# An expert layer's fixed first pass: 64 and 32 rows picked by products, in place of 128 gathered rows

## The chip, the cores and the metric

The kernel runs on one core of a Trainium2 chip. The metric is the device time of one execution in microseconds; a median of a few runs is given, and beside it the time of one execution that the hardware profiler took.

## The reference

Two layers run one after the other on a sequence of 512 tokens of width 1024, all in fp32. The first is a gated mixer (two causal convolutions, a linear recurrence, an output projection). The second adds 16 meta tokens, runs two kinds of attention, projects, and normalises; then comes the part that matters here, a mixture of 32 experts with four experts for each token:

```python
logits = h @ w_router + b_router
top_val, top_idx = lax.top_k(logits, 4)
gates = jax.nn.softmax(top_val, axis=-1)
# for each token and each of its four experts e:
hgu = h[tok] @ w_gate_up[e] + b_gate_up[e]          # 1024 -> 2048
glu, lin = minimum(hgu[::2], 7), clip(hgu[1::2], -7, 7)
act = glu * sigmoid(1.702 * glu) * (lin + 1)
out[tok] += gate * (act @ w_down[e] + b_down[e])    # 1024 -> 1024
```

A last layer norm over the residual and this sum gives the output. Every expert has 8 MB of gate-up and 4 MB of down weights, and all 32 experts are read.

## The kernel before, in words

**Order of the work.** The kernel is written with a manual schedule: each engine runs its instructions in the order in which the program emits them. After attention, an output projection (the loop over `hf` and `i`, around L1466) writes the residual rows `hr` in four blocks of 128 tokens. Beside it each block is normalised (`stats1`, `norm1`, `affine1`), written to DRAM as `h1_d` and `acc_d`, and the router's logits and the four best experts are found (`logits_T`, `logits`, `top4`). Products of the selection with a triangle give each token's place within its expert (`posb`) and the experts' counts; `Pk` orders the experts by count, and `pm_i` holds the order as whole numbers, from which SP reads the addresses of the weights.

**Passes.** Experts are worked through in 32 passes. Pass 0 is always expert 0 (`STATIC`), so its weights can be loaded before the order is known. Passes 3 and 9 (`PAIRS`) take the two largest experts in two tiles of 128 and 32 rows; the next largest have 128 rows, the passes in `SMALL` 64 and those in `TINY` 32. What does not fit is done by a loop at the end (`further_tiles`). A pass has eight gate-up units and four down units, each one load of 1 MB. The down units of pass b - 1 follow the gate-up units of pass b; functions listed by `beside(b)` run before (`before`) or in the middle of (`midst`) the unit with their number: `place`, `fetch` and `gather` find and fetch the rows of the next pass, `xpose` and `xparts` transpose them, `glu`, `at_T` and `at_parts` make the activation and its transpose, `finish` scales and scatters.

**Precision.** A tile of 128 rows uses weights split into two fp32r parts, high and low (ScalarE copies, VectorE subtracts, L142 and L143), and three products for each (L1930, L1941). Tiles of 64 and 32 rows use the raw fp32 weights, with the columns of the array divided in two or four (`small_products`, L1912).

**Weights and buffers.** `Weights` keeps a list of loads in order and a list of free raw buffers of 1 MB. `split` turns a raw buffer into a split one (there are three, of two halves each) and frees the raw one, whereupon the next load is issued on SP; a raw unit frees its buffer with `release` after its products. In the expert stage there are twelve raw buffers, three of which lie where the router's tiles lay before and become free with them.

**Pass 0 before the change.** A one-hot of expert 0's places (`onehot`) times the token numbers gives the indices (`rows_at`); `rows_of` gathers the 128 rows from `h1_d` by an indirect DMA; `xpose` and `xparts` transpose and split them. Twelve warming products of no use (`warm`) stand ahead of the transposes on TensorE. `order()` permutes places and gates by the order of the experts, in steps after the units of pass 0; `late_gates` then finds the gates of pass 0.

Of the kernel before, what the change touches and what calls it, by code (L numbers as in the profile page):

```python
# [9 lines left out]
F32 = mybir.dt.float32  # L10
# [4 lines left out]
OP = mybir.AluOpType  # L15
# [4 lines left out]
S = 512  # L20
# [14 lines left out]
STATIC = 1  # L35
PAIRS = (3, 9)
# [5 lines left out]
def _tables():  # L42

    f = np.float32
    inv = (f(10000.0) ** (-np.arange(0, 64, 2, dtype=f) / f(64))).astype(f)
    pos = np.concatenate([np.arange(NM, NK), np.arange(NM)]).astype(f)
    t = np.arange(S)
    row = np.concatenate([t // 64, np.full(NM, -1)]).astype(f)
    col = np.concatenate([t % 64, np.arange(NM)]).astype(f)

    def block(p):
        ang = (p[None, :] * inv[:, None]).astype(f)
        c, s = np.cos(ang).astype(f), np.sin(ang).astype(f)
# [24 lines left out]
    for r, q_ in enumerate([*PAIRS, *large, *[q_ for q_ in SMALL if q_ not in TINY], *TINY, *range(STATIC)]):  # L78
        moe[:, q_] = r
        moe[:, 32 + q_] = 160 if q_ in PAIRS else 32 if q_ in TINY else 64 if q_ in SMALL else 128  # L80
    moe[:, 64] = p // 64
    moe[:, 65] = p // 32

    least = np.arange(NE) + 131072.0 * (np.arange(NE) < STATIC)
    moe[:, 66] = least[p % NE]
    moe[:, 67:67 + NE] = least

    moe[:64, 68 + NE] = moe[64:, 70 + NE] = 1.0
    return {"t_rope": np.ascontiguousarray(rope.astype(f)), "t_sq": sq, "t_moe": moe}


class Weights:
# [3 lines left out]
    def __init__(self, nc, pools, slots):  # L96
        self.nc, self.slots = nc, list(slots)
        self.parts = [(pools, f"wpart{i}") for i in range(2)]
        self.todo, self.raw, self.part = [], [], []
        self.last, self.used = 0, 0  # L100

    def add(self, *loads, split=True, n=2048, pieces=1, late=0):

# [44 lines left out]
        self.rest = [lambda i=i: piece(i) for i in range(1, pieces)]  # L148

    def release(self, slot):  # L150
        self.slots.append(slot)
        self.issue()

    def ahead(self, n):
        while len(self.part) < n and self.ready():
# [15 lines left out]
def block_kernel(ctx, tc, A, out, dbg=None, upto=99):  # L171
# [118 lines left out]

    PASSES, ni = [], 0
    for p in range(NE):
        k = 1 + (p in PAIRS)
        PASSES.append(list(range(ni, ni + k)))
        ni += k
    NI = ni
# [8 lines left out]

    def paired(p):

        return p not in PAIRS and p not in TINY
# [4 lines left out]
    def add_unit(p, dn, u, of, late=0):  # L313
        def src():
            w = of(p)[dn]
            return rows2(w[256 * u:256 * u + 256, :], paired(p)) if dn else w[128 * u:128 * u + 128, :]
        W.add((kn(2, 1024) if dn else flat, src), split="both" if p in PAIRS else p not in SMALL,
              late=late)

    def add_block(b, of):  # L320
# [1143 lines left out]
    for hf in range(2):  # L1464
        sl_ = slice(512 * hf, 512 * hf + 512)
        wb = [t.rearrange("p (k n) -> p k n", k=4) for t in W.get(1)]  # L1466
        wa = [t.rearrange("p (k n) -> p k n", k=4) for t in W.get(0)]
        for i in range(4):
            pa, pb = psa("pwa"), psa("pwb")
            for g, p_, w in ((1, pb, wb), (0, pa, wa)):  # L1470
                for k in range(4):
                    mm3(p_, [t[:, 4 * g + k, 128 * i:128 * i + 128] for t in osp], [t[:, k, :] for t in w], k == 0, k == 3)
                if hf and i and g:
                    logits_T(i - 1)
                    norm1(i - 1)
            if hf and i:
                logits(i - 1)
            if hf == 0 and i == 0:
                o_scales()
                l1g = bcast(A["ln1_g_2"], pB, "hm")  # L1480
            for g, p_ in ((1, pb), (0, pa)):
                dve.scalar_tensor_tensor(out=hr[:, i, sl_], in0=p_, scalar=rst[:, i, g:g + 1], in1=hr[:, i, sl_],
                                         op0=OP.mult, op1=OP.add)
                if hf and i and g:
                    affine1(i - 1)
            if hf:
                stats1(i)
                if i:
                    top4(i - 1)
                else:  # L1490
                    W.ahead(1)
            elif i == 1:
                biases()
            elif i == 2:
                W.ahead(1)
                next(terms)
            elif i == 3:
                next(terms)
    logits_T(3)
    norm1(3)  # L1500
    logits(3)
# [53 lines left out]
        dve.tensor_copy(out=pi2[:, c0:c1], in_=pi_[:, c0:c1])  # L1555
        return pi2

    def rows_of(pi_, nt=1):
# [9 lines left out]
        w = 128 // nt  # L1568
        xg = xg2[nsl[0] % 2][0:w]
        nsl[0] += 1  # L1570
        pool.indirect_dma_start(out=xg, out_offset=None, in_=h1_d[:, :],  # L1571
                                in_offset=bass.IndirectOffsetOnAxis(ap=ix[0:w], axis=0),
                                bounds_check=S - 1, oob_is_err=False)
# [7 lines left out]
        dve.scalar_tensor_tensor(out=gt, in0=pi_[:, 2:3], scalar=pi_[:, 3:4], in1=pi_[:, 4:5], op0=OP.add, op1=OP.add)  # L1581
        return gt

    oh_ = onehot(posb[:, :, 0:1])
    first = rows_of(rows_at(oh_, lambda i: aux[:, :, i, 0], 0, 2))

    cnt = pK.tile([128, NE], F32, name="cnt")
    pmr = pK.tile([128, NE], F32, name="pmr")
# [178 lines left out]
    def small(n):  # L1767

        if PASS_OF[n] in TINY or PLACES[n][1]:
            return 4  # L1770
        return 2 if PASS_OF[n] in SMALL else 0

    def place(n):
        p, k = PLACES[n]
        pl = posb[:, :, p:p + 1]
        if k:
            pl2 = pM.tile([128, 4], F32, tag="pl2", name="pl2", bufs=2)
            dve.tensor_scalar(out=pl2, in0=posb[:, :, p], scalar1=128.0, scalar2=None, op0=OP.subtract)
            pl = pl2.unsqueeze(2)
        its[n] = {"oh": onehot(pl, small(n) or 1), "cols": lambda i: aux[:, :, i, p], "se": selr[:, p:p + 1].to_broadcast([128, 128]),  # L1780
                  "acc": {}, "ac": {}, "pa": {}, "parts": {}}
# [21 lines left out]
                                         in1=it["pi"][:, 1:2], op0=OP.add, op1=OP.add)  # L1803
        it["gt"] = gates_of(it["pi"])

    def late_gates(n):
        it = its[n]
        it["gt"] = gates_of(rows_at(it["oh"], it["cols"], 2, 5))

    def xpose(n):  # L1810
        it = its[n]
        if small(n):
            it["pt"] = transposed_rows(it["xg"])
        else:
            pt = pss("pxt") if n == 0 else None
            it["pt"] = [transposed(it["xg"], a, pt[:, a, :] if n == 0 else psa("pxt")) for a in range(2)]

    def x_tile():
        return [pM.tile([128, 8, 128], F32R, tag=t, name=t) for t in ("xTh", "xTl")]
# [72 lines left out]
    def small_products(n, dn, u, w, half):  # L1892
# [15 lines left out]
        for k in range(2):  # L1908
# [38 lines left out]
    def beside(b):  # L1947
# [21 lines left out]
                before[9 if b else 8].append((glu, n, 1))  # L1969
        nxt = PASSES[b + 1] if b + 1 < NE else []  # L1970
        if b == 0:
            before[4].append((place, 1))
            midst[4].append((fetch, 1))
            before[5] += [(gather, 1), (late_gates, 0)]
            before[8].append((place, 2))
            midst[7].append((xpose, 1))
            before[8].append((xparts, 1))
        else:
            for j, n in enumerate(nxt):
                if j:  # L1980
# [27 lines left out]
    def further_tiles():  # L2008
# [4 lines left out]
        with tc.For_i(0, total, 1) as it:  # L2013
            with tc.manual_schedule():
# [46 lines left out]

    W.slots += [(pM, f"wraw{RAW + RAWK + i}") for i in range(RAWX)]
    W.prefetch()
    its[0] = {"oh": oh_, "cols": lambda i: aux[:, :, i, 0], "ix": first[0], "xg": first[1],
              "se": selr[:, 0:1].to_broadcast([128, 128]), "acc": {}, "ac": {}, "pa": {}, "parts": {}}
    for p, dn, u in units(1):
        if not dn:
            add_unit(p, dn, u, of, -4)
# [129 lines left out]
```

## Time and profile before

| | |
|---|---|
| median of three runs (lowest to highest) | 1894.53 us (1890.97 to 1894.7) |
| profiled execution | 1889.37 us, span 1887.6 us |
| granted TensorE clock, mean | 0.951 |
| busy: TensorE, VectorE, ScalarE, GpSimd | 1682.0, 1127.2, 752.8, 512.6 us |
| first load of pass 0's weights, first product of pass 0 | 752.96, 819.84 us |
| last load of weights issued | 1831.34 us |

The span runs from the first to the last instruction. Rows of the timeline give the start of a group of equal instructions, its length, its engine (SPq is SP's queue of transfers), its line and operation, the tiles it writes and reads, the shapes and a count. Behind them in brackets stands the time for which the engine was idle before, and what ended that. A matmul of fp32 operands leaves two records, and a record's length includes its way through the array, so the pace of a stream is read from start to start. A granted clock of 1.00 is 2.4 GHz and 0.50 is 1.2 GHz.

### The profile page before, as it was taken

The numbers are of one execution on the slowest core, as the hardware profiler recorded it, in microseconds if no ns is written. First come the engines' busy times: TensorE is split into PE (matmuls) and PEld (weight loads), VectorE is DVE, ScalarE is ACT, GpSimd is POOL, SyncE is SP. The second block draws the span as 40 slices with busy tenths as digits, with TensorE's granted clock in tenths as the row PEclk, the third lists the DMA queues.
The fourth block names the chain that finished last, engine by engine and source line by source line (L and its number), as shares of the span: only waits on it lengthen the run. The fifth ranks groups of instructions, "written<-read, shape, count | busy, mean of one in ns | idle before, by whom it ended". The sixth has DMA issues, their size and how long they took to land. (4 is left out here: it accounts for less than half of the span.)

```text
span 1887.6 us, 22807 instructions
## 1 busy us (share of the span) xinstructions
PE 1682.0 (89%) x8479; PEld 1120.8 (59%) x8479; DVE 1127.2 (60%) x1467; ACT 752.8 (40%) x894; POOL 512.6 (27%) x400
## 2 busy tenths in 40 slices
PE   4899785979998899978999999999999999999885
PEld 3687573758787677854565565666456556642221
DVE  6799983775746555756565466566547545641113
ACT  5233542742335545333354354445335534520001
POOL 3899994550311221311111101110011011110102
PEclk8999897989999899989899999999999999999998
DMA  8322221336131003769999999999999999999993
GB/s 300 90 73 73 78 90 45 111 133 210 59 109 56 1 1 111 296 266 364 379 394 410 399 413 397 394 403 414 418 404 407 406 404 393 405 407 397 407 414 136
DMA packets 127442, 503.49 MB, mean 267 GB/s; under 512 B 15227, under 2 KB 57785, under 8 KB 79713
## 3 DMA queue, kind: packets, MB, share of 16 engines
q1 hardware_dynamic: 115568, 475.24, 63.7%
q0 software_dynamic: 11024, 25.39, 4.9%
q8 instruction: 68, 1.11, 0.2%
q10 hardware_dynamic: 736, 1.38, 0.2%
q14 instruction: 46, 0.37, 0.1%
HBM read 488.56 MB, written 19.84 MB: 269 GB/s over the span
## 5 line engine op out<-in xcount | busy, mean ns | idle before, releaser
L143 DVE TENSOR_TENSOR wlo<-wraw,whi 128x2048 fp32r<-128x2048 f32 (+1 forms) x201 | 456.9, 2282 | 177.8 <-ACT whi L142 172.1
L142 ACT CAST whi<-wraw 128x2048 fp32r<-128x2048 f32 (+1 forms) x201 | 379.5, 1890 | 222.2 <-DMA wraw<-w_down 93.9
L1912 PE MATMUL pg<-wraw,xTs 128*64 128x512 f32 (+1 forms) x1664 | 277.1, 518 | 15.0 <-DMA wraw<-w_gate_up 14.8
L1912 PEld LDWEIGHTS pg<-wraw,xTs 128*64 128x64 f32 (+1 forms) x1664 | 85.5, 126 | 166.2 <-issue 109.8
L1912 PE MATMUL pg<-wraw,ats 128*64 128x512 f32 (+1 forms) x832 | 146.2, 527 | 8.9 <-DMA wraw<-w_down 6.7
L1660 DVE TENSOR_SCALAR lp<-pg 128x512 f32<-128x512 f32 (+1 forms) x47 | 31.1, 661 | 191.9 <-ACT sg L1659 190.3
L563 POOL TENSOR_TENSOR acc<-acc,sparel 128x512 f32<-128x512 f32 x91 | 133.3, 1465 | 7.7 <-ACT acc L552 0.2
L1667 POOL DMA_INDIRECT acc_d<-y,back x20 | 33.1, 1656 | 374.9 <-ACT y L1886 357.1
L1571 POOL DMA_INDIRECT xg<-h_d,ix x34 | 53.9, 1584 | 235.3 <-PE pg L1912 109.8
L1930 PE MATMUL pg<-whi,xTh 128*128 128x512 f32 x416 | 117.1, 403 | 0.4 <-issue 0.4
L1930 PE MATMUL pg<-whi,xTl 128*128 128x512 f32 x416 | 115.8, 400 | 0.0
L1930 PE MATMUL pg<-wlo,xTh 128*128 128x512 f32 x416 | 113.3, 394 | 0.0
L1667 POOL DMA_INDIRECT acc_d<-y,ix x13 | 26.1, 2011 | 309.0 <-ACT y L1889 210.2
L556 DVE SCALAR_TENSOR_TENSOR pc<-v,C,pc 128x512 f32<-128x512 f32 x144 | 101.6, 747 | 2.1 <-ACT pc L552 0.8
L1659 ACT ACTIVATE sg<-pg 128x512 f32<-128x512 f32 (+1 forms) x47 | 25.7, 573 | 183.4 <-PE pg L1912 99.9
L561 POOL TENSOR_SCALAR sparel<-v,C 128x512 f32<-128x512 f32 x91 | 93.8, 1031 | 14.5 <-DVE V L478 5.8
L1930 PEld LDWEIGHTS pg<-whi,xTh 128*128 128x128 f32 x416 | 76.3, 189 | 26.5 <-issue 10.3
L1930 PEld LDWEIGHTS pg<-wlo,xTh 128*128 128x128 f32 x416 | 78.9, 190 | 17.9
L1930 PEld LDWEIGHTS pg<-whi,xTl 128*128 128x128 f32 x416 | 77.3, 190 | 16.6
L1941 PE MATMUL pg<-whi,ath 128*128 128x512 f32 x208 | 73.9, 438 | 12.8 <-ACT whi L142 12.8
L1912 PEld LDWEIGHTS pg<-wraw,ats 128*64 128x64 f32 (+1 forms) x832 | 41.2, 127 | 73.7 <-issue 47.6
L1941 PE MATMUL pg<-wlo,ath 128*128 128x512 f32 x208 | 71.7, 428 | 11.8 <-DVE wlo L143 11.8
(661 smaller groups left out, 3289.3 us busy)
## 6 DMA issues: line engine op xcount, KB each, us to landing
wraw<-w_gate_up SPq DMA_DIRECT2D x256, 1024.0 KB, 20.5
wraw<-w_down SPq DMA_DIRECT2D x128, 1024.0 KB, 21.7
wraw<-w_in SPq DMA_DIRECT2D x17, 1024.0 KB, 5.3
wraw<-w_out SPq DMA_DIRECT2D x8, 1024.0 KB, 6.1
mraw<-mod_w SPq DMA_DIRECT2D x7, 1024.0 KB, 12.5
wraw<-w_in SPq DMA_DIRECT2D x14, 512.0 KB, 5.1
wraw<-pw_w SPq DMA_DIRECT2D x4, 1024.0 KB, 5.2
wraw<-mod_w SPq DMA_DIRECT2D x4, 1024.0 KB, 5.1
```

Source lines behind the costliest of these rows:

```text
L142: self.nc.scalar.copy(out=hi[:, c], in_=t[:, c])
L143: self.nc.vector.tensor_tensor(out=lo[:, c], in0=t[:, c], in1=hi[:, c].bitcast(F32), op=OP.subtract)
L556: dve.scalar_tensor_tensor(out=acc[:, c, :] if j == 29 and not np_ else st_["o"], in0=v[:, j:j + S], scalar=dw_col(j, c), in1=st_["o"], op ...
L561: pool.tensor_scalar(out=pr_, in0=v[:, j:j + S], scalar1=dw_col(j, c), scalar2=0.0, op0=OP.mult, op1=OP.add)
L563: pool.tensor_tensor(out=acc[:, c, :], in0=acc[:, c, :], in1=pr_, op=OP.add)
L1571: pool.indirect_dma_start(out=xg, out_offset=None, in_=h1_d[:, :], in_offset=bass.IndirectOffsetOnAxis(ap=ix[0:w], axis=0), bounds_check=S ...
L1659: act.activation(out=sg, in_=v2[:, :, :, 0], func=AF.Sigmoid, scale=1.702)
L1660: dve.tensor_scalar(out=lp, in0=v2[:, :, :, 1], scalar1=-6.0, scalar2=8.0, op0=OP.max, op1=OP.min)
L1667: pool.indirect_dma_start(out=dst, out_offset=bass.IndirectOffsetOnAxis(ap=ix, axis=0), in_=y, in_offset=None, bounds_check=nt * S - 1, oo ...
L1912: pe.matmul(o, l, t[:, c0:c0 + n_], start=False, stop=u == 3 and k == 1 if dn else u == 7)
L1930: pe.matmul(it["acc"][c // 2][:, c % 2, :], l, r[:, 512 * c:512 * c + 512], start=False, stop=u == 7 and j == 2)
L1941: pe.matmul(it["acc"][2][:, c, :], l, r[:, c0:c0 + 512], start=False, stop=end)
```

## The change

Pass 0 gets two tiles, of 64 and of 32 rows, with raw weights. The limit of expert 0 falls from 128 to 96 rows; what is over goes to the loop at the end. Its rows are no longer gathered: a one-hot of 96 places in fp32 is the moving operand of 32 products, with the normalised rows in `hr` as weights, which give the rows of pass 0 already transposed. The first eight of these products stand ahead of the two products that make the experts' order, the other 24 behind them. ScalarE copies the result into two tiles. `late_rows` finds the scatter addresses and gates of both tiles before unit 3. As pass 0 is not split, `lend` adds the six halves of the split buffers to the free raw buffers after the projection's loop; they are not returned to the list when they are released. A pass of two tiles releases its raw buffer after the second.

```diff
+    def lend(self):
+        self.lent = [(pool, tag + x) for pool, tag in self.parts for x in "hl"]
+        self.slots += self.lent
+        self.prefetch()
...
-        k = 1 + (p in PAIRS)
+        k = 1 + (p in PAIRS or p < STATIC)
...
+    W.lend()
     logits_T(3)
     norm1(3)
...
-    oh_ = onehot(posb[:, :, 0:1])
-    first = rows_of(rows_at(oh_, lambda i: aux[:, :, i, 0], 0, 2))
+    oh0 = xg2[0][:, 0:4 * 96].rearrange("p (i n) -> p i n", i=4)
+    dve.tensor_tensor(out=oh0, in0=iotab[:, 0:96].unsqueeze(1).to_broadcast([128, 4, 96]),
+                      in1=posb[:, :, 0:1].to_broadcast([128, 4, 96]), op=OP.is_equal)
+    first = pss("first")
+    def pick_rows(ks):
+        for k in ks:
+            for i in range(4):
+                pe.matmul(first[:, k // 4, 96 * (k % 4):96 * (k % 4) + 96], hr[:, i, 128 * k:128 * k + 128], oh0[:, i, :],
+                          start=(i == 0), stop=(i == 3))
+    pick_rows(range(2))
...
     pe.matmul(pp1[:, NE:2 * NE], pcol[0:NE, 1:2].to_broadcast([NE, 128]), Pk[0:NE], start=True, stop=True)
+    pick_rows(range(2, 8))
...
-    def late_gates(n):
+    def late_rows(n):
         it = its[n]
-        it["gt"] = gates_of(rows_at(it["oh"], it["cols"], 2, 5))
+        place(n)
+        fetch(n)
+        it["gt"], it["ix"] = gates_of(its[n]["pi"]), rows_of(its[n]["pi"], small(n), False)[0]
+        its[n] = it
...
-        W.release(slot)
+        if n == PASSES[PASS_OF[n]][-1]:
+            W.release(slot)
...
-            before[5] += [(gather, 1), (late_gates, 0)]
+            before[5].append((gather, n1))
+            before[3] += [(late_rows, 0), (late_rows, 1)]
...
     warm(12, bias_p)
-    xpose(0)
-    xparts(0)
+    for n, (tag, c0, w) in enumerate((("xTh", 0, 64), ("xTs", 64, 32))):
+        xp = pM.tile([128, 8, w], F32, tag=tag, name="xTs")
+        act.copy(out=xp.rearrange("p (a k) w -> p a k w", a=2),
+                 in_=first[:, :, 0:4 * 96].rearrange("p a (k w) -> p a k w", k=4)[:, :, :, c0:c0 + w])
```

## Rows read from the trace of the kernel before

**Rows 1.** Windows of the expert stage: us, engines' busy time, PEclk, DMA share, GB/s.
```profile
820.00:860.00 40.00, 34.93 (x258) 25.59 (x259) 23.48 (x38) 17.18 (x15) 3.76 (x2) 0.96 0.65 247
...
1200.00:1400.00 200.00, 191.47 (x897) 116.73 (x889) 117.83 (x123) 89.37 (x79) 21.19 (x13) 0.97 1.02 410
```

**Rows 2.** Windows around the end of pass 3, the same columns.
```profile
934.00:946.00 12.00, 10.49 (x63) 5.00 (x65) 6.31 (x11) 1.84 (x4) 0.00 (x0) 1.00 0.78 279
946.00:960.00 14.00, 13.72 (x163) 7.26 (x160) 6.62 (x10) 8.02 (x11) 2.68 (x2) 1.00 1.02 368
```

**Rows 3.** Timeline of SP's queue: a row write, a down load, a later load.
```profile
800.67 0.32 SPq L1423 DMA_DIRECT2D h_d<-hr  x1
...
810.59 0.33 SPq L117 DMA_DIRECT2D wraw<-w_down  x1
...
937.95 0.33 SPq L117 DMA_DIRECT2D wraw<-w_gate_up  x1
```

**Rows 4.** Timeline of TensorE: pass 0, its end, its down units.
```profile
819.84 1.17 PE L1930 MATMUL pg<-whi,xTh 128*128 128x512 f32 x4 [0.38 <-issue]
...
822.66 1.10 PE L1930 MATMUL pg<-whi,xTh 128*128 128x512 f32 x4
...
844.49 0.68 PE L1645 MATMUL pxt<-sq,xg 32*128 32x32 f32 x8 [2.70 <-DMA xg<-h_d,ix]
...
848.18 1.05 PE L1906 MATMUL pg<-bias_p,se 128*128 128x256 f32 x4
...
860.74 0.72 PE L1941 MATMUL pg<-whi,ath 128*128 128x512 f32 x2
...
866.38 0.68 PE L1645 MATMUL pxt<-sq,xg 64*128 64x64 f32 x8 [1.25 <-DMA xg<-h_d,ix]
...
874.26 0.62 PE L1906 MATMUL pg<-bias_p,se 128*128 128x512 f32 x2
```

**Rows 5.** Timeline of TensorE: passes of 32 and 64 rows, one unit of pass 3.
```profile
855.43 4.96 PE L1912 MATMUL pg<-wraw,xTs 128*32 128x256 f32 x88
...
881.99 7.95 PE L1912 MATMUL pg<-wraw,xTs 128*64 128x512 f32 x36
...
917.95 1.20 PE L1930 MATMUL pg<-whi,xTh 128*128 128x512 f32 x4
...
921.90 1.20 PE L1930 MATMUL pg<-whi,xTh 128*128 128x512 f32 x4
```

**Rows 6.** Timeline of TensorE: narrow products, warming, the entry to pass 3.
```profile
787.42 1.87 PE L1443 MATMUL plog<-rw,xg 128*128 128x32 f32 x16
...
810.66 5.01 PE L198 MATMUL warm<-bias_p 128*128 128x512 f32 x12
...
898.16 1.06 PE L1645 MATMUL pxt<-sq,xg 32*128 32x32 f32 x8 [3.35 <-DVE xTl L215]
899.14 1.94 PE L1912 MATMUL pg<-wraw,ats 128*32 128x256 f32 x16
```

**Rows 7.** Windows of TensorE alone: us, busy time, PEclk, DMA share, GB/s.
```profile
802.00:814.00 12.00, 5.75 (x43) 0.50 0.65 229
814.00:816.00 2.00, 2.00 (x10) 0.75 1.00 414
848.00:850.00 2.00, 1.87 (x13) 0.72 0.00 0
906.00:908.00 2.00, 2.00 (x8) 0.71 1.01 423
```

**Rows 8.** Timeline of VectorE: the first one-hot, indices of two gathers.
```profile
805.04 0.69 DVE L1546 TENSOR_TENSOR oh<-sq,posb 128x512 bf16<-128x512 f32 x1
...
835.68 0.15 DVE L1566 CAST ix<-tok 128x1 int32<-128x1 f32 x1
...
856.56 0.15 DVE L1566 CAST ix<-tok 128x1 int32<-128x1 f32 x1
```

**Rows 9.** Timeline of ScalarE: the first split for pass 3.
```profile
891.75 1.90 ACT L142 CAST whi<-wraw 128x2048 fp32r<-128x2048 f32 x1 [1.17 <-DMA wraw<-w_gate_up]
```

More of the change, by code (lines that the diff above doesn't have):

```diff
@@ L79, in _tables @@
         moe[:, q_] = r
-        moe[:, 32 + q_] = 160 if q_ in PAIRS else 32 if q_ in TINY else 64 if q_ in SMALL else 128
+        moe[:, 32 + q_] = 160 if q_ in PAIRS else 32 if q_ in TINY else 64 if q_ in SMALL else 96 if q_ < STATIC else 128
     moe[:, 64] = p // 64
@@ L99, in __init__ @@
         self.todo, self.raw, self.part = [], [], []
-        self.last, self.used = 0, 0
+        self.last, self.used, self.lent = 0, 0, []
     def add(self, *loads, split=True, n=2048, pieces=1, late=0):
@@ L150, in release @@
     def release(self, slot):
-        self.slots.append(slot)
-        self.issue()
+        if slot not in self.lent:
+            self.slots.append(slot)
+            self.issue()
+    def lend(self):
+        self.lent = [(pool, tag + x) for pool, tag in self.parts for x in "hl"]
+        self.slots += self.lent
+        self.prefetch()
     def ahead(self, n):
@@ L306, in paired @@
     def paired(p):
-        return p not in PAIRS and p not in TINY
+        return p not in PAIRS and p not in TINY and p >= STATIC
     def rows2(w, pairs):
@@ L316, in src @@
             return rows2(w[256 * u:256 * u + 256, :], paired(p)) if dn else w[128 * u:128 * u + 128, :]
-        W.add((kn(2, 1024) if dn else flat, src), split="both" if p in PAIRS else p not in SMALL,
+        W.add((kn(2, 1024) if dn else flat, src), split="both" if p in PAIRS else p not in SMALL and p >= STATIC,
               late=late)
@@ L1556, in rows_at, with rows_of @@
         return pi2
-    def rows_of(pi_, nt=1):
+    def rows_of(pi_, nt=1, gather=True):
         ix = pK.tile([128, 1], I32, tag="ix", name="ix", bufs=6)
@@ L1567, in rows_of @@
             back = pK.tile([128, 1], I32, tag="back", name="back", bufs=6)
[L1568 to L1573, printed above, removed]
+        xg = None
+        if gather:
+            w = 128 // nt
+            xg = xg2[nsl[0] % 2][0:w]
+            nsl[0] += 1
+            pool.indirect_dma_start(out=xg, out_offset=None, in_=h1_d[:, :],
+                                    in_offset=bass.IndirectOffsetOnAxis(ap=ix[0:w], axis=0),
+                                    bounds_check=S - 1, oob_is_err=False)
         if nt > 1:
@@ L1770, in small @@
             return 4
-        return 2 if PASS_OF[n] in SMALL else 0
+        return 2 if PASS_OF[n] in SMALL or PASS_OF[n] < STATIC else 0
     def place(n):
@@ L1777, in place @@
             pl2 = pM.tile([128, 4], F32, tag="pl2", name="pl2", bufs=2)
-            dve.tensor_scalar(out=pl2, in0=posb[:, :, p], scalar1=128.0, scalar2=None, op0=OP.subtract)
+            dve.tensor_scalar(out=pl2, in0=posb[:, :, p], scalar1=64.0 if p < STATIC else 128.0, scalar2=None,
+                              op0=OP.subtract)
             pl = pl2.unsqueeze(2)
@@ L1814, in xpose @@
         else:
-            pt = pss("pxt") if n == 0 else None
-            it["pt"] = [transposed(it["xg"], a, pt[:, a, :] if n == 0 else psa("pxt")) for a in range(2)]
+            it["pt"] = [transposed(it["xg"], a, psa("pxt")) for a in range(2)]
     def x_tile():
@@ L1971, in beside @@
         if b == 0:
-            before[4].append((place, 1))
-            midst[4].append((fetch, 1))
-            before[5] += [(gather, 1), (late_gates, 0)]
-            before[8].append((place, 2))
-            midst[7].append((xpose, 1))
-            before[8].append((xparts, 1))
+            n1, n2 = PASSES[1][0], PASSES[2][0]
+            before[4].append((place, n1))
+            midst[4].append((fetch, n1))
+            before[5].append((gather, n1))
+            before[3] += [(late_rows, 0), (late_rows, 1)]
+            before[8].append((place, n2))
+            midst[7].append((xpose, n1))
+            before[8].append((xparts, n1))
         else:
@@ L2063, in block_kernel @@
     W.prefetch()
-    its[0] = {"oh": oh_, "cols": lambda i: aux[:, :, i, 0], "ix": first[0], "xg": first[1],
-              "se": selr[:, 0:1].to_broadcast([128, 128]), "acc": {}, "ac": {}, "pa": {}, "parts": {}}
+    for n in PASSES[0]:
+        its[n] = {"acc": {}, "ac": {}, "pa": {}, "parts": {}}
+        selectors(n)
     for p, dn, u in units(1):
@@ L2074, in block_kernel @@
     warm(12, bias_p)
-    xpose(0)
-    xparts(0)
+    for n, (tag, c0, w) in enumerate((("xTh", 0, 64), ("xTs", 64, 32))):
+        xp = pM.tile([128, 8, w], F32, tag=tag, name="xTs")
+        act.copy(out=xp.rearrange("p (a k) w -> p a k w", a=2),
+                 in_=first[:, :, 0:4 * 96].rearrange("p a (k w) -> p a k w", k=4)[:, :, :, c0:c0 + w])
+        for k in range(8):
+            its[n]["parts"][0, k] = xp[:, k]
     for b in range(NE + 1):
```

## The prediction, made before the changed kernel ran

> **What bounds the kernel now.** I read the windows first. From 1200 to 1400 us the sixteen DMA engines are busy at a share of 1.02 and move 410 GB/s [rows 1]: the expert stage is a stream of 1 MB weight loads, one per 1.05 MB / 410 GB/s = 2.56 us. At its head there is a hole: share 0.65 and 247 GB/s from 820 to 860 [rows 1]. The change aims at this hole, so the question is whether a microsecond saved there survives to the end.
>
> The second view is the windows of the place where pass 3 ends. The share is 0.78 from 934 to 946 and 1.02 from 946 on [rows 2]. Ahead of 946 every load that could be issued has landed: the queue row at 937.95 [rows 3] comes as a unit of TensorE ends and releases its buffer. So there all twelve weight buffers are full and the loads are paced by TensorE. Pass 3 makes 3.95 us of TensorE work per load (917.95 to 921.90 [rows 5]) against 2.56 us of transfer: here the DMA queue catches up whatever it lost before. Behind 946 the stream has a fixed length. The end of the kernel is then the end of pass 3 on TensorE plus that stream, and what counts ahead of it is TensorE's own chain from the router to pass 3.
>
> **The change part by part.** Times stand against the profiled execution, 1889.37 us (span 1887.6). The median of the runs is 1894.53, 5.2 us higher, and the result is carried over to it.
>
> *Lent buffers.* Six halves of the split buffers become raw buffers at the end of the projection. The loads for them stand in SP's queue behind a row write of the first layer norm at 800.67 [rows 3], so they start at about 801: the three outstanding down loads, of which the last two went at 810.59 and just after [rows 3], and then, once the expert order is known, six loads of pass 1 where three were possible. Pass 0 frees its eight buffers as its units end. By the end of its gate-up pass 6 + 8 = 14 loads of later passes are issued, against 8 before: a lead of 6 x 2.56 = 15 us of transfer. The lent buffers (three with weights of pass 1, three with down units) are not refilled, so at the start of pass 2 both kernels have the same twelve loads ahead, and the lead turns into idle DMA ahead of 934. TensorE's waits between 820 and 934 are on gathers and on VectorE, none on a weight load, so I cost this at nothing; if that is wrong it is the first rival.
>
> *Rows by products.* Removed: a one-hot, four small products, the first gather and its landing, eight transposes and two splits. Added: a one-hot of 4 x 96 and 32 fp32 products of 128x128 by 96, two records each: 64. The one-hot is ready where the old one was, about 805.6 (805.04 plus three quarters of 0.69 [rows 8]). No row shows this shape. The nearest has 128x128 fp32 weights and 32 columns, 16 records in 1.87: 0.117 each [rows 6]. At half clock a record costs twice that: sixteen narrow records took 1.94 at 899.14 [rows 6] where 88 took 4.96 [rows 5], 0.121 against 0.056. The clock is at half when the products begin, 0.50 from 802 to 814 [rows 7].
> The first 16 records: 16 x 0.234 = 3.7, to 809.4. The expert order's two products wait behind them and take about 1.0, to 810.4; the expert numbers are about 1 us later, hidden since pass 1 is not wanted before 848. Then 48 records. The clock rose at 815, 4.3 us after TensorE set to work at 810.66, at 849.1, 4.6 us after 844.49, and once only 9 us after 898.16 [rows 4, 6, 7]. From 805.65 that makes 810 to 815. With the early rise they take 48 x 0.117 = 5.6, to 816.0; with the late one 18 x 0.234 + 30 x 0.117 = 7.8, to 818.2. Behind them stand two transposes (0.2), the twelve warming products, now at full clock (2.8, as a unit of twelve [rows 4]), and pass 0's bias (0.5); the copies of the picked rows lie beside the warming. First gate-up product: 819.5 to 821.7, where it was 819.84 [rows 4], so -0.3 to +1.9. I take +0.5, since two of three rises were early.
>
> *Pass 0 in 64 and 32 rows.* Before, a unit is twelve products, 2.8 us (819.84 to 822.66 [rows 4]). For 64 rows it is 8 records: 36 took 7.95 [rows 5], 1.72 for 8 from start to start. For 32 it is 16 records, 0.90 at 0.056 each; but in pass 3, where they alternate with a wide tile, a unit is 3.95, and 3.95 - 2.8 = 1.15 [rows 5]. I take 1.72 + 1.18 = 2.9. So TensorE does not become faster, though the rows are fewer.
> The Trainium skill, TensorEngine Tiling (Array Packing), section Key Properties, says that a change of tiling mode drains the engine. Each new unit changes mode twice, so this rule speaks against the change; by it a unit is 2.9, without it 2.62 and the gate-up pass 2.2 us shorter. The trace agrees, with 1.15 against 0.90 [rows 5].
> Eight units are 23.2. Added: the second tile's bias 0.65, order products 0.4, three index products 0.75, transposes of pass 1 0.7. The late rows stand before unit 3: their second one-hot waits for some nine short VectorE operations behind the first index product, about 1.7 us of idle TensorE. The gather of pass 1 is asked for at unit 4: its indices are ready 17.4 after the first product. From the indices to the data it took 8.7 (835.83 to 844.49) and the next gather 9.7 (856.71 to 866.38) [rows 4, 8]. So the data are there at 26.1 to 27.1; TensorE comes for them at 25.6, and after the transposes and the last share of 32 the pass ends at 28.0 to 29.0. Before: 819.84 to 848.18, 28.3, with a wait of 2.70 for the same gather [rows 4]. I take 28.5: +0.2 (-0.3 to +0.7). The splits of pass 0 on ScalarE and VectorE are gone; they hid beside TensorE, and what they cost it stands in the next part.
>
> *Pass 1 and pass 0's down units.* The swiglu of two tiles is one behind the other on VectorE, and the 64 comes second: its transpose waits about 1.8 where it waited 0.4; a wait of 1.4 on a split goes, and the copy of pass 1's rows is 0.3 later: +0.3 (0 to +1). The four down units took 13.5, 860.74 to 874.26, with a wait of 1.25 for a gather [rows 4]. Now the products are 4 x 2.9 in place of 4 x 2.8, the bias 0.2 longer, and the wait goes, since the indices of pass 2 no longer stand behind splits: -0.7 (-1.5 to 0).
>
> *Entry to pass 3.* TensorE waits 3.35 at 898.16 for VectorE [rows 6], and the clock is at half until 907 [rows 7]. ScalarE's split before it waited 1.17 for a weight load [rows 9], which now lies ready; but VectorE has other work until it takes that split up. I cost it at 0 (-7.5 to 0).
>
> **Sum:** 0.5 + 0.2 + 0.3 - 0.7 + 0 = +0.3. Profiled 1889.7, median 1894.8: no change.
>
> **The rivals.**
> 1. The lead counts. If the stage is bound by the stream from 813 on, the holes close: 0.35 x 40 = 14.0 [rows 1], 0.22 x 12 = 2.6 [rows 2], and two loads that are there before the order is known, 2 x 2.56 = 5.1: 21.7 in all, 1873. For it: 900 us at full share. Against it: the full buffers of rows 2. Chance 0.12.
> 2. Late weights set the entry to pass 3. With its loads landed early the splits begin earlier, VectorE is free, and the wait of 3.35 and the low clock behind it go (the records of 1.94 and more between 898 and 907 lose some 4 us): -7.5, 1887. For it: the wait of 1.17 on a load just ahead [rows 9]. Against it: VectorE's queue there holds other work. Chance 0.15.
> 3. The clock stays low through picking and warming. Then 64 x 0.234 = 15.0, the order 1.0, transposes 0.4, warming 5.0 as at 810.66 [rows 6], bias 0.9: pass 0 starts at 827.9, +8.1, and the median is 1902. It decides if the rise comes later than about 818. For it: the rise that took 9 us. Against it: picking gives TensorE work almost without a pause. Chance 0.12, with smaller delays of the same kind.
> 4. The change doesn't do what it says: the lent loads wait in SP's queue and start only at 810 with the others. By the argument above that costs nothing and falls into my forecast.
>
> **How the numbers follow.** Forecast 0.61, rivals 0.12, 0.15 and 0.12. What a measurement of this kernel can tell from no change is about 0.2%, 3.8 us. The ends of the forecast's terms add up to -2.1 and +3.6 around nothing, 1892.4 to 1898.1, its own range; for parts of rivals 2 and 3 I leave 0.05 of it below -3.8 and 0.06 above +3.8, 0.50 between. Faster 0.12 + 0.15 + 0.05 = 0.32, same 0.50, slower 0.12 + 0.06 = 0.18. The range takes in rival 2 and all but the end of rival 3, and leaves out rival 1: 1881 to 1901.
>
> **What would show it.** Right: three loads from about 801; more idle DMA between 865 and 946 than now; units of pass 0 of 2.9; a wait on VectorE before unit 3; pass 3's first wide product within 2 us of 903.4, where it is now; the stream after it unchanged. Wrong: a DMA share near 1 from 813 through 946 with the end much earlier (rival 1), no wait ahead of pass 3 (rival 2), a granted clock of 0.5 past 818 (rival 3), or any wait of TensorE on a weight load ahead of 934.

## The result and the profile after

| | before | after |
|---|---|---|
| median of four runs each, same chip | 1892.75 us | 1908.22 us |
| ratio, 95% interval | | 1.0085 (1.0061 to 1.0109) |
| profiled execution, span | 1889.37 us, 1887.6 | 1906.01 us, 1904.2 |

The changed kernel is slower by some 16 us. Forecast was no change, with a range that ended at 1901: the prediction was wrong.

The work ahead of the experts takes a little longer or shorter from one execution to the next, so both profiles are read from one anchor, the last group of logits products: 799.17 before, 800.69 after. TensorE before: the anchor, the first products of pass 2, the end of pass 2 and the first wide product of pass 3 (the columns are start, length, engine, line, operation, tiles, shape, count, and in brackets the idle time ahead and what ended it):

```profile
799.17 1.97 PE L1443 MATMUL plog<-rw,xg 128*128 128x32 f32 x16 [0.73 <-ACT xg L1436]
...
874.82 1.08 PE L1912 MATMUL pg<-wraw,xTs 128*64 128x512 f32 x4
...
889.86 0.50 PE L1906 MATMUL pg<-bias_p,se 128*128 128x256 f32 x2
...
903.37 2.07 PE L1930 MATMUL pg<-whi,xTh 128*128 128x512 f32 x4
```

TensorE after, the start of pass 0:

```profile
800.69 1.97 PE L1450 MATMUL plog<-rw,xg 128*128 128x32 f32 x16 [0.73 <-ACT xg L1443]
...
807.26 3.70 PE L1603 MATMUL first<-xg,hr 128*128 128x96 f32 x16 [1.71 <-DVE cnt L1615]
...
811.88 7.78 PE L1603 MATMUL first<-xg,hr 128*128 128x96 f32 x48
820.73 0.33 PE L1708 MATMUL pord<-sq,posb 128*128 128x128 f32 x1 [1.07 <-ACT xTs L2107]
...
820.92 2.99 PE L205 MATMUL warm<-bias_p 128*128 128x512 f32 x12
...
824.31 1.94 PE L1938 MATMUL pg<-wraw,xTs 128*64 128x512 f32 x8
```

From the anchor to the first wide product of pass 0 it is 23.62 us, where it was 20.67 (819.84 in [rows 4]). The 64 picks took 11.5 us. TensorE, passes 0 and 1 and the down units of pass 0:

```profile
836.18 0.26 PE L1561 MATMUL pidx<-aux,oh 128*128 128x5 bf16 x4 [1.70 <-DVE oh L1550]
836.38 6.44 PE L1938 MATMUL pg<-wraw,xTs 128*64 128x512 f32 x32
...
857.45 0.66 PE L1697 MATMUL pat<-sq,ac 128*128 128x128 f32 x2 [2.01 <-DVE ac L1684]
...
867.24 1.94 PE L1938 MATMUL pg<-wraw,ats 128*64 128x512 f32 x8
```

The wait for the late rows (1.70) is there, and the gather waits of 2.70 and 1.25 [rows 4] are gone. Behind the wait the granted clock stood at half from 837.0 to 840.4, and the 32 records there took 6.44; in experiment 7, behind the same wait with the clock up, they took 4.80. TensorE's window (us, busy time, granted clock, DMA share, GB/s):

```profile
837.00:840.00 3.00, 3.00 (x16) 0.50 0.89 374
```

TensorE from pass 2 to pass 3:

```profile
880.64 1.08 PE L1938 MATMUL pg<-wraw,xTs 128*64 128x512 f32 x4
...
895.27 0.27 PE L1561 MATMUL pidx<-aux,oh 128*128 128x5 bf16 x4 [7.58 <-DVE oh L1550]
895.47 9.38 PE L1938 MATMUL pg<-wraw,xTs 128*64 128x512 f32 x36
904.78 0.50 PE L1932 MATMUL pg<-bias_p,se 128*128 128x256 f32 x2
...
913.08 1.06 PE L1667 MATMUL pxt<-sq,xg 32*128 32x32 f32 x8 [4.34 <-DVE xTl L222]
...
918.29 2.07 PE L1957 MATMUL pg<-whi,xTh 128*128 128x512 f32 x4
```

Here is the loss. In the middle of pass 2 TensorE stands for 7.58 us, in a place where it did not wait at all before, and the 36 records behind it, which took 7.95 [rows 5], take 9.38, since the granted clock fell to half from 891.6 to 898.4. What VectorE and GpSimd did at that time:

```profile
891.58 0.19 DVE L1739 TENSOR_TENSOR xy<-cnt,moe 128x32 f32<-128x32 f32 x1 [12.34 <-DMA acc_d<-y,back]
...
894.52 0.69 DVE L1550 TENSOR_TENSOR oh<-sq,pl 128x512 bf16<-128x512 f32 x1
```

```profile
880.38 1.63 POOL L1689 DMA_INDIRECT acc_d<-y,back  x1 [18.32 <-issue]
885.07 1.57 POOL L1689 DMA_INDIRECT acc_d<-y,back  x1 [3.06 <-DMA acc_d<-y,back]
```

`xy` is the scratch in which the arithmetic for the loop at the end (`further()`) begins. It is allocated under the buffer name `yt`. Before the change nothing used that buffer while pass 0's result was being scattered. Now pass 0 has a second, 32-row tile, and `finish` puts the scaled rows of such a tile into `yt`. So the first small step of `further()` waits until the scatter of these rows has left the buffer: the second of two scatters, which itself waits 3.06 us for the first to land. VectorE works in order, so it stood for 12.34 us, with the one-hot for which TensorE waits behind it in its queue.

SP's queue and the DMA windows of the changed kernel (columns: stretch, length, each engine's busy time, granted clock, DMA share, GB/s):

```profile
802.18 0.32 SPq L1430 DMA_DIRECT2D h_d<-hr  x1
802.60 1.83 SPq L117 DMA_DIRECT2D wraw<-w_down  x3
806.39 0.82 SPq L1430 DMA_DIRECT2D h_d<-hr  x2
807.25 0.94 SPq L1432 DMA_DIRECT2D acc_d<-hr  x2
814.16 7.14 SPq L117 DMA_DIRECT2D wraw<-w_gate_up  x6
```

```profile
810.00:840.00 30.00, 27.23 (x177) 16.98 (x180) 7.14 (x31) 2.51 (x4) 0.00 (x0) 0.84 1.00 403
...
850.00:860.00 10.00, 7.40 (x66) 3.08 (x63) 3.94 (x7) 1.77 (x5) 0.00 (x0) 0.87 0.69 270
...
890.00:900.00 10.00, 4.73 (x20) 1.65 (x22) 7.74 (x22) 0.00 (x0) 1.97 (x2) 0.66 0.43 157
...
960.00:975.00 15.00, 14.72 (x168) 7.58 (x165) 6.70 (x11) 7.87 (x11) 2.68 (x2) 1.00 1.01 373
```

The lending does what it says: the hole from 820 [rows 1] is full up to 840, and the DMA engines idle later instead, in stretches between 840 and 960 (shares of 0.69 and 0.43 in the lines above), until pass 3 has ended.

### The profile page after: what moved, and what is told of

Read it like the earlier page. It is cut to its first block, busy times and chain, and to the rows that moved or that the text cites. A ratio compares the mean times of both kernels' runs of the same rounds, so it can differ in the third digit from the quotient of the medians.

```text
span 1904.2 us, 23177 instructions
## 1 busy us (share of the span) xinstructions
PE 1700.7 (89%) x8680; PEld 1114.0 (58%) x8680; DVE 1103.3 (58%) x1462; ACT 729.5 (38%) x883; POOL 510.1 (27%) x400
## 5 line engine op out<-in xcount | busy, mean ns | idle before, releaser
L143 DVE TENSOR_TENSOR wlo<-wraw,whi 128x2048 fp32r<-128x2048 f32 (+2 forms) x189 | 433.7, 2303 | 169.9 <-ACT whi L142 157.4
L142 ACT CAST whi<-wraw 128x2048 fp32r<-128x2048 f32 (+2 forms) x189 | 356.8, 1889 | 203.5 <-DMA wraw<-w_down 85.5
L1938 PE MATMUL pg<-wraw,xTs 128*64 128x512 f32 (+1 forms) x1856 | 305.1, 519 | 15.6 <-DMA wraw<-w_gate_up 14.8
L1938 PEld LDWEIGHTS pg<-wraw,xTs 128*64 128x64 f32 (+1 forms) x1856 | 93.5, 127 | 183.2 <-issue 124.4
L1938 PE MATMUL pg<-wraw,ats 128*64 128x512 f32 (+1 forms) x928 | 157.7, 519 | 9.6 <-DMA wraw<-w_down 7.1
L1957 PE MATMUL pg<-whi,xTh 128*128 128x512 f32 x384 | 108.0, 403 | 0.0
L1957 PE MATMUL pg<-whi,xTl 128*128 128x512 f32 x384 | 107.7, 402 | 0.0
L1957 PE MATMUL pg<-wlo,xTh 128*128 128x512 f32 x384 | 104.9, 395 | 0.0
L1689 POOL DMA_INDIRECT acc_d<-y,ix x12 | 23.6, 1966 | 288.0 <-ACT y L1915 184.5
L1957 PEld LDWEIGHTS pg<-wlo,xTh 128*128 128x128 f32 x384 | 72.4, 189 | 17.1
L1968 PE MATMUL pg<-wlo,ath 128*128 128x512 f32 x192 | 66.5, 429 | 12.7 <-DVE wlo L143 12.7
L1968 PE MATMUL pg<-whi,ath 128*128 128x512 f32 x192 | 67.2, 433 | 8.9 <-ACT whi L142 8.9
## 6 DMA issues: line engine op xcount, KB each, us to landing
wraw<-w_down SPq DMA_DIRECT2D x128, 1024.0 KB, 21.4
```

The lines of the kernel that those rows point to most:

```text
L142: self.nc.scalar.copy(out=hi[:, c], in_=t[:, c])
L143: self.nc.vector.tensor_tensor(out=lo[:, c], in0=t[:, c], in1=hi[:, c].bitcast(F32), op=OP.subtract)
L1689: pool.indirect_dma_start(out=dst, out_offset=bass.IndirectOffsetOnAxis(ap=ix, axis=0), in_=y, in_offset=None, bounds_check=nt * S - 1, oo ...
L1957: pe.matmul(it["acc"][c // 2][:, c % 2, :], l, r[:, 512 * c:512 * c + 512], start=False, stop=u == 7 and j == 2)
L1968: pe.matmul(it["acc"][2][:, c, :], l, r[:, c0:c0 + 512], start=False, stop=end)
```

## The experiments

The table is read from each kernel's TensorE timeline: from the anchor to the first wide product of pass 0, to that of pass 3, and from there to the end of the span.

| kernel | to pass 0 | to pass 3 | pass 3 to end | ratio to before (95%) |
|---|---|---|---|---|
| before | 20.7 | 104.2 | 984.2 | 1 |
| after | 23.6 | 117.6 | 985.9 | 1.0085 (1.0061 to 1.0109) |
| 1 own scratch | 23.5 | 107.4 | 983.4 | 1.0022 (1.0012 to 1.0032) |
| 2 before, the wait alone | 20.5 | 111.8 | 982.5 | 1.0039 (1.0026 to 1.0053) |
| 3 before, delay ahead of pass 2 | 20.6 | 108.1 | 983.5 | 1.0019 (1.0007 to 1.0031) |
| 4 before, delay ahead of pass 5 | 20.5 | 102.3 | 983.3 | 0.9994 (0.9982 to 1.0005) |
| 5 before, picking alone | 26.3 | 109.9 | 987.1 | 1.0035 (1.0020 to 1.0049) |
| 6 own scratch, rows gathered | 27.0 | 111.3 | 983.8 | 1.0041 (1.0024 to 1.0058) |
| 7 own scratch, no warming | 21.4 | 103.8 | 984.7 | 0.9999 (0.9983 to 1.0016) |
| 8 own scratch, three lent | 23.5 | 108.0 | 984.9 | 1.0010 (0.9999 to 1.0022) |
| 9 as 7, clock held up | 22.3 | 108.2 | 983.5 | 1.0018 (1.0005 to 1.0031) |
| 10 as 9, second tile later | 22.8 | 104.9 | 983.1 | 1.0011 (1.0000 to 1.0021) |
| 11 as 10, lent behind the row writes | 17.3 | 97.8 | 985.1 | 0.9983 (0.9971 to 0.9995) |
| 12 as 7, lent behind the row writes | 21.6 | 103.6 | 984.9 | 1.0015 (1.0002 to 1.0027) |

From pass 3 to the end it is 982.5 to 987.1 us in all fourteen, whatever was done ahead of it, while the time to pass 3 moves by 20 us. The times are of one profiled execution each, and they scatter: experiment 4 has the program of the kernel before up to pass 3, and it came there 1.9 us earlier. Most of that lies in the entry to pass 3 (from the end of pass 2's gate-up units to the first wide product), which took 11.3 to 13.5 us in the fourteen.

**1. Own scratch.** The changed kernel with one name altered:

```diff
-        xy = pM.tile([128, 256], F32, tag="yt", name="xy")
+        xy = pM.tile([128, 256], F32, tag="ats", name="xy")
```

> The changed kernel, with the scratch tile of the further-tiles arithmetic in another buffer than the scaled rows of the second tile. Theory A (the wait on that buffer costs): VectorE's wait of 12.3 us for the scatter and TensorE's of 7.6 us behind it go, and the half clock after them; pass 2's gate-up units take 15 us again in place of 24, and the kernel is 9 us faster than the changed one, 1899 (some 6 above the kernel before). Rival B (the new pass 0 is slow in itself, by its fp32 products and the picking): the wait moves somewhere else, 1906 to 1908.

Measured: 1895.52 us, ratio 1.0022; some 12 of the 16 us are back. The same step on VectorE, and TensorE behind it:

```profile
882.54 0.20 DVE L1739 TENSOR_TENSOR xy<-cnt,moe 128x32 f32<-128x32 f32 x1 [0.87 <-PE pg L1938]
```

```profile
890.06 0.26 PE L1561 MATMUL pidx<-aux,oh 128*128 128x5 bf16 x4
890.25 7.95 PE L1938 MATMUL pg<-wraw,xTs 128*64 128x512 f32 x36
```

The 12.34 are 0.87, the 7.58 are gone and the 36 records take 7.95 again. The shared buffer is the cause of most of the loss. Pass 2 is 9.1 us shorter; the other 3 lie in the entry to pass 3 (12.6 for 13.5) and in the stream behind it (983.4 for 985.9), and since single executions differ by as much, their cause stays open.

**2. The wait alone, in the kernel before.** At the same place a write of 32 columns to the buffer `y`, which there holds the rows being scattered:

```diff
+                if b == 2 and j == 0:
+                    yw = pM.tile([128, 1024], F32, tag="y", name="yw")
+                    dve.memset(yw[:, 0:32], 0.0)
                 next(lists, None)
```

> The kernel before, with one short VectorE write into the buffer of pass 0's scaled rows, ahead of the same arithmetic in pass 2: VectorE must wait until the scatter from that buffer has landed, some 12 us. Theory A: TensorE waits for the one-hot behind it, 7 to 10 us, and all of it comes out at the end: 1900 to 1903. Rival B: VectorE has slack there, and the stream of loads sets the end: 1893.

Measured: 1897.72 us, ratio 1.0039, so some 7 us, the low end of what was expected. VectorE and TensorE:

```profile
887.77 0.09 DVE L2122 MEMSET yw<- 128x32 f32 x1 [11.25 <-DMA acc_d<-y,ix]
```

```profile
891.47 0.27 PE L1553 MATMUL pidx<-aux,oh 128*128 128x5 bf16 x4 [6.21 <-DVE oh L1542]
```

An instruction of 0.09 us that waits 11.25 in VectorE's queue makes a tuned kernel 0.4% slower.

**3 and 4. A delay of TensorE, early and late.** The kernel before, with twenty products of no use ahead of one pass:

```diff
+            if b == 2 and j == 0:     # 4: b == 5
+                warm(20, bias_p)
             run(before[j])
```

> The kernel before, with 20 more warming products (4.65 us of TensorE at full clock) ahead of pass 2. Theory A (TensorE's chain to the end of pass 3 sets the end): +4.6 us, 1897.4. Rival C (the stream of loads sets the end from the start of the expert stage): no change, 1893.

> The kernel before, with the same 20 products ahead of pass 5. Theory A: TensorE has slack behind pass 3, as the loads set the pace there: 0 to +1 us, 1893. If TensorE set the pace all the way: +4.6.

Measured: 1895.08 us ahead of pass 2 (ratio 1.0019), 1889.08 ahead of pass 5 (0.9994). The twenty took 4.75 us ahead of pass 2, and pass 3 came 3.9 us later. Ahead of pass 3 TensorE's time is the kernel's time, and two passes later the same work is free. This is the prediction's idea of what sets the end, and it holds.

**5. Picking alone.** The kernel before with the 128 rows of its pass 0 picked by 32 products of 128 columns, then split as before; nothing lent, no tiles:

```diff
-    first = rows_of(rows_at(oh_, lambda i: aux[:, :, i, 0], 0, 2))
...
+    first = pss("first")
...
+    def pick_rows(ks):
...
+    pick_rows(range(2))
...
+    pick_rows(range(2, 8))
```

> The kernel before (128 rows, split weights, no lent buffers) with the rows of pass 0 picked by 32 products on 128 columns in place of the first gather and its transposes. Theory A (TensorE's chain counts, and picking at half clock with the warming behind it starts pass 0 later): first product of pass 0 some 3 us later, the end 3 us later, 1894 to 1895. Rival: picking takes the trip through DRAM out of the chain, pass 0 starts earlier, 1888 to 1890.

Measured: 1899.17 us, ratio 1.0035, more than expected. TensorE:

```profile
815.39 5.62 PE L1597 MATMUL first<-xg,hr 128*128 128x128 f32 x48
823.98 0.30 PE L1702 MATMUL pord<-sq,posb 128*128 128x128 f32 x1 [2.96 <-DVE xTl L215]
...
824.14 4.50 PE L198 MATMUL warm<-bias_p 128*128 128x512 f32 x12
```

The picked rows lie in PSUM, and the order's products next on TensorE need that room: they wait until the picked rows have been read out, 2.96 us with splits and 1.07 with plain copies. With the splits the clock fell behind that pause (a mean of 0.82 from 824 to 826, 0.50 from 826 to 828), and the warming took 4.50 where the changed kernel's took 2.99.

**6. Tiles and lending, but rows gathered.** Experiment 1 with the old gather and eight transposes in place of the picks:

```diff
-    first = pss("first")
...
-    pick_rows(range(2))
+    first = rows_of(rows_at(onehot(posb[:, :, 0:1]), lambda i: aux[:, :, i, 0], 0, 2))
```

> The changed kernel with its own scratch buffer, and pass 0's 96 rows gathered and transposed as before, in place of picked. Theory A: pass 0 starts 3 us earlier than with picked rows, and the end comes 3 us earlier: 1892.5, within 1.5 of the kernel before. Rival (the rest of the 4 us is in the tiles of 64 and 32): no gain, 1895.5.

Measured: 1901.08 us, ratio 1.0041, where a gain on experiment 1 was expected. GpSimd, TensorE and SP's queue:

```profile
820.37 1.12 POOL L1581 DMA_INDIRECT xg<-h_d,ix  x1 [11.91 <-DMA h_d<-hr]
```

```profile
828.45 1.97 PE L1660 MATMUL pxt<-sq,xg 128*128 128x128 f32 x8 [7.79 <-DMA xg<-h_d,ix]
```

```profile
806.12 1.82 SPq L117 DMA_DIRECT2D wraw<-w_down  x3
809.90 0.81 SPq L1430 DMA_DIRECT2D h_d<-hr  x2
```

The gather reads what the last row writes put down, and these are issued behind three lent loads of 1 MB. It went at 820.37, 16.2 us behind the anchor (804.21); before it went at 808.42, 9.3 behind. So the two halves of the change belong together: lending at that place makes a gather late, and picking is what avoids it.

**7. No warming.** Experiment 1 without `warm(12, bias_p)`.

> The changed kernel with its own scratch buffer and without the twelve warming products. Theory A: the picking has brought the clock up, so the 2.8 us of warming are only a delay: 1892.5. Rival: the wait for ScalarE's copies of the picked rows, which the warming covers, takes its place, or the clock falls again: 1895 or more.

Measured: 1891.59 us, ratio 0.9999. The warming products stood behind picks that had already worked TensorE for 11 us, and without them pass 0 starts 2.1 us earlier; there they were a delay. Pass 3 comes 3.6 us earlier. Of the other 1.5, 1.4 lie in the gate-up units of pass 0 (27.4 us for 28.8): the wait for the late rows is the same, but in this execution the clock stayed up behind it:

```profile
831.86 4.80 PE L1938 MATMUL pg<-wraw,xTs 128*64 128x512 f32 x32
```

It stayed up in experiments 6 and 12 too, and fell there in 1, 8 and 9 as in the changed kernel. What decides that, no run tells.

**8. Half the lending.** Experiment 1 with `self.lent` cut to its first three buffers.

> The changed kernel with its own scratch buffer, with three lent buffers in place of six: pass 1 then has three loads under way when the order is known, as in the kernel before. Theory A (a lead of the loads ahead of pass 3 is worth nothing): no change against six, 1895.5. Rival C (the stream counts): three loads later, 3 x 2.56 = 7.7 us, 1903.

Measured: 1893.03 us, ratio 1.0010. Three loads of lead less cost nothing that can be seen.

**9 and 10. The clock held up for the picks.** Experiment 7 with 19 products of 128x512 on a bank of their own (`fill`) in TensorE's waits ahead of the picks; 10 also works out the second tile's places three units later:

```diff
+    fill(3)
     logits(3)
...
+            if i > 1 and j == i:
+                fill(i + 2)
...
+    fill(7)
     pick_rows(range(2))
...
-            before[3] += [(late_rows, 0), (late_rows, 1)]      # 10 alone
+            before[3].append((late_rows, 0))
+            before[6].append((late_rows, 1))
```

> The kernel without the twelve warming products, plus 19 dummy products of 128x512 on a bank of their own in the waits of TensorE ahead of the picking: 3 before the last logits products, 4 and 5 before the two position products that wait for VectorE, 7 before the first pick. Theory (the chain from the router to the end of pass 3 sets the end, and 64 picks at the half clock took 11.4 us of it): if the dummies keep the granted clock at 1.0, 64 picks take about 64 x 0.113 = 7.2 us, the chain is 3 to 4 us shorter than without them, and the time is 1887 to 1889, ratio to the kernel before 0.998 (0.997 to 0.999). Rival 1 (the clock falls all the same): the picks keep their 11.4 us and the dummies, 0.40 us each, push the position products back by 1 to 3 us: 1892 to 1895, ratio 1.000 to 1.002. Rival 2 (the chain at the start no longer decides, since the order and the gate products wait for ScalarE's copies and for a weight load): the picks are faster and the first wide product of pass 0 starts no earlier: 1891, ratio 1.000.

> The same dummies, and the place of the second tile of the fixed pass is worked out three units later than that of the first (unit 6 in place of unit 3), so that its one-hot is not waited for by TensorE. Theory: the wait of 1.70 us before the second pidx products of pass 0 goes, and as the chain decides, all of it is seen at the end: 1.7 us below the kernel with the dummies alone, 1885 to 1887, ratio 0.997 (0.996 to 0.998). Rival 1: the 1.70 us come back at the next wait of the chain (the transposes at the start of pass 1 wait for VectorE's ac, which now has the second tile's work ahead of it): as with the dummies alone, within 0.5 us. Rival 2 (the clock falls all the same): 1.7 us below 1892 to 1895.

Measured: 1893.95 us (ratio 1.0018) and 1891.10 (1.0011). TensorE and ScalarE of 9:

```profile
806.87 2.00 PE L1612 MATMUL first<-xg,hr 128*128 128x96 f32 x16
...
809.35 5.60 PE L1612 MATMUL first<-xg,hr 128*128 128x96 f32 x48
820.67 0.47 PE L1718 MATMUL pord<-sq,posb 128*128 128x128 f32 x1 [5.72 <-ACT xTs L2116]
...
822.53 3.68 PE L1948 MATMUL pg<-wraw,xTs 128*64 128x512 f32 x8
```

```profile
819.75 0.86 ACT L2116 COPY xTs<-first 128x512 f32<-128x512 f32 x2 [15.59 <-DMA wraw<-w_gate_up]
```

The dummies kept the clock at 1.0 and the picks took 7.6 us in place of 11.5, as the theory had it, and nothing came of it. That is the second rival, though with another cause, which experiment 11 tests: the copy of the picked rows on ScalarE began at 819.75, almost 5 us behind the last pick, VectorE and SP's next load went at the same moment, and in the pause the clock fell, so that the first products of pass 0 ran at half of it. In the changed kernel the picks end at 819.66 and the copy begins at 819.82: there the second floor was hidden behind the slow picks. In 10 the wait of 1.70 went, and with it the half clock behind it (32 records took 6.47 in 9 and 4.80 in 10); the median fell by 2.9 us.

**11 and 12. The lent loads behind the row writes.** The copy goes into room that the rows `hr` occupied; it is free when their last writes to DRAM have landed, and on SP's queue these stood behind the lent loads. The row of the copy in 9 names a weight load as what ended the wait, but by the semaphore times of that trace this load landed only at 821.95, and the last of the row writes at 819.50, 0.25 us ahead of the copy. One line is moved, in 10 and in 7:

```diff
-    W.lend()
     logits_T(3)
...
     affine1(3)
+    W.lend()
```

> The kernel with the dummies and the later second tile, with the call that lends the six buffers moved behind the last row writes of the first half (four writes of 256 and 512 KB each, 1.5 MB together), so that the three loads that it starts stand behind these writes on SP's queue and no longer ahead of them. Theory: the picks ended at 813.5 there and ScalarE's copy of them began at 818.83, because it writes into room that the first half's rows give free only when their writes have landed, and these stood behind three loads of 1 MB. With the writes ahead the copy begins within 0.5 us of the last pick, the first wide product of pass 0 starts 5 us earlier and at the full clock, and all of that is seen at the end: 1883 to 1887, ratio 0.997 (0.996 to 0.998). Rival 1 (the lead of the loads counts after all): three loads and those behind them land 4 to 5 us later and the second and third pass wait for them: 1891 to 1895. Rival 2 (the copy waits for something else, such as a weight load): the copy begins at the same distance from the logits and the time is as before the move, ratio 1.001.

> The kernel without the twelve warming products (no dummies, the second tile worked out where the change has it), with the same move of the lending call alone. Theory: there the picks run at the half clock and end at about the time at which the row writes land, so each of the two hides the other, and taking away the late landing alone gives at most 1 us: 1890 to 1892, ratio 0.9995 (0.998 to 1.001). Rival (the late landing is the only floor): the copy begins 3 us or more earlier, 1887 to 1889.

Measured: 1886.69 us, ratio 0.9983 (0.9971 to 0.9995), and 1892.71, ratio 1.0015. SP's queue, ScalarE and TensorE of 11:

```profile
805.31 5.04 SPq L1430 DMA_DIRECT2D h_d<-hr  x3
810.40 0.94 SPq L1432 DMA_DIRECT2D acc_d<-hr  x2
811.43 2.98 SPq L117 DMA_DIRECT2D wraw<-w_down  x3
```

```profile
818.66 0.86 ACT L2117 COPY xTs<-first 128x512 f32<-128x512 f32 x2 [10.95 <-DMA wraw<-w_down]
```

```profile
812.91 5.60 PE L1612 MATMUL first<-xg,hr 128*128 128x96 f32 x48
819.58 0.33 PE L1718 MATMUL pord<-sq,posb 128*128 128x128 f32 x1 [1.07 <-ACT xTs L2117]
...
821.06 1.94 PE L1948 MATMUL pg<-wraw,xTs 128*64 128x512 f32 x8
```

The copy follows the last pick by 0.15 us, pass 0 starts 17.3 us behind the anchor (20.7 before, 22.8 in 10) and pass 3 starts 6.4 earlier than in the kernel before, though 2.2 of these lie in the entry to pass 3, which scatters by as much. This version is a little faster than both kernels: 3.4 us under the one before and, by the two ratios, 1.0% under the changed one. In 12, with the clock low, the same move alone brings nothing: the slow picks still hold the copy. Its ratio lies just above what was expected (0.998 to 1.001) and 0.16% above experiment 7's, but the two intervals overlap and the two profiles agree within 0.2 us up to pass 3 and behind it. Whether the loads that start later cost anything stays open.

## Why the prediction was wrong

**What sets the end: right.** TensorE's chain from the router to the end of pass 3 plus a fixed stream. The stream was 985.9 us long against 984.2; pass 3 came 13.4 us later behind the anchor, and the end some 16. Experiments 3, 4 and 8 show it from both sides: time on the chain counts, lead of the loads does not. Rival 1 (the lead) falls with it, and rival 2 too: the weights lay ready (TensorE waited for none from 815 to 975), and yet the entry to pass 3, from 904.78 to 918.29, took 13.51 us, exactly as before (889.86 to 903.37), with the wait for VectorE still in it (4.34). That is as costed, but the exactness is luck: experiment 4, the same program as before up to there, took 11.9.

**Where the sum failed: a step that is not in it.** The prediction followed pass 0's second tile through its gate-up and down units and stopped there. That a second tile also has its rows scaled and scattered, out of which buffer, and who else uses that buffer, was not asked. The term is +9.1 us: from 880.64 to 904.78 is 24.1, where pass 2 took 15.0 (874.82 to 889.86). Of it 7.58 are the wait and 1.4 the half clock behind it. Experiment 1 takes it out, and experiment 2 puts such a wait into the other kernel.

**The terms that were in the sum** came to +4.2 us in place of +0.3, which experiment 1 measures at the end: +4 us.

- Picking and the start of pass 0: +2.95, where +0.5 was taken out of -0.3 to +1.9. The clock rose at 816.5, so the picks went as in the late case: 12.4 us from the start of the first to the end of the last (807.26 to 819.66), where the late case had 12.5 (805.65 to 818.2). Two of three rises in the trace had been early, and that was a poor reason to choose the early one. The 1.05 us above the range is the wait of the order's products for the copy of the picked rows (1.07), a sharing of PSUM that the range left out. "The copies lie beside the warming" was therefore wrong: they lie ahead of it.
- Gate-up of pass 0: 28.9 us (824.31 to 853.16) against 28.5 forecast and 28.3 before. That it came out so near is luck, two errors against each other. The wait of 1.7 for the late rows was foreseen, the half clock behind it was not, and it cost 1.6 (6.44 for 4.80). The gather that was to set the end of the pass was no wait at all: the products that need it ran at 851.55 without a pause. A unit of both tiles takes 2.87 (843.95 to 846.82), where 2.9 was worked out. The rule of the Trainium skill (TensorEngine Tiling (Array Packing), section Key Properties) that a change of tiling mode drains the engine had spoken for 2.9 against 2.62; the trace agrees with it here too.
- Pass 1: +1.5, where +0.3 was taken out of 0 to +1. It took 14.1 us (853.16 to 867.24) against 12.6 (848.18 to 860.74). The waits that were foreseen came out a little larger, 2.01 and 0.59. Here too the sum had no half clock behind a wait: it stood at 0.50 from 858 to 860 and cost some 1.2 us, estimated from 32 records that took 3.2 us there and 2.0 at full clock before.
- Down units of pass 0: -0.8, forecast at -0.7 (12.7 us, 867.24 to 879.97, against 13.5).

**Rival 3** (the clock low through picking and warming) was the right place and half right: the clock was at half for the picks up to 816.5. Its price was too high by what the rise gave back. Behind it, unseen, lay a second floor of nearly the same height: the row writes delayed by the lent loads. Rival 4 said that late lent loads would cost nothing. What it did not ask is what the early ones push back in the queue.

## What to carry to other kernels

When a change gives a tile to a pass that had none, follow it to its last instruction, and at each buffer name ask who else allocates it: a 0.2 us step behind a scatter blocked VectorE for 12 us and cost 9 on the path. Before making a step faster, look for what would have been late at the same moment; here the slow picks of the changed kernel ended 19.0 us behind the anchor, the late row writes held the copy until 19.5 behind it in experiment 9, and only removing both gained. Price a wait of TensorE together with the clock that it may cost behind it. Loads put early into a queue are paid for by what stood behind them, even where their own lead is worth nothing.

## What the hardware showed that was not expected

- The two indirect scatters of pass 0, which add to the same tensor, ran one after the other: the second was issued 4.69 us after the first, 3.06 of them a wait for the first to land, and a buffer was free some 6.5 us after its own scatter's start (885.07 to 891.58).
- A pause of TensorE can be paid twice. Behind the wait of 7.58 us the same 36 records took 9.38 in place of 7.95, and behind that of 5.72 in experiment 9 eight records took 3.68 in place of 1.94. Behind a wait of 1.70 the clock fell in four kernels (the changed one, 1, 8 and 9: 32 records in 6.44 to 6.47) and stayed up in three (6, 7 and 12: 4.80 to 4.81).
- 64 fp32 records with 96 columns took 11.5 us while the granted clock was mostly 0.5, and 7.6 with it at 1.0. At 1.0 the number of columns made no difference: 48 records took 5.60 with 96 columns and 5.62 with 128 (experiment 5), 0.117 each, the pace that the prediction had taken from 32 columns.
